# Alternating feed-forward blocks: another order within a step on TensorE, VectorE and ScalarE, squares one step later, forms at steps 9 to 20

## The chip, the cores and the metric

The kernel runs on one core of a Trainium2 chip. The metric is the device time of one execution in microseconds. A change of less than about 0.2% can't be told from none.

## What is computed

The reference is one encoder block: two gated mixing branches, an output projection and a layer norm, then a feed-forward part with a second layer norm. The change lies in the feed-forward part alone:

```python
ff = jnp.square(jax.nn.relu(h @ w_ff1[l])) @ w_ff2[l]
h = _layernorm(DEEPNORM_ALPHA * h + ff, ln2_g[l], ln2_b[l])
```
h is 256 x 2048, w_ff1 is 2048 x 8192, w_ff2 is 8192 x 2048, all float32. The kernel gets its precision by splitting each float32 operand into a high part (a cast to fp32r) and a low part (the rest), and by multiplying high x high, high x low and low x high.

## The kernel before

The hidden width of 8192 is cut into four quarters of 16 blocks of 128 channels. `ff1_first` (L1210) computes the first quarter's hidden blocks. `ff_pairs` (L1278) then runs 48 **steps** (SLOTS). Each step does two things: it computes one hidden block of the next quarter (tile f: 2048 input channels times 128 hidden channels, for 256 tokens), and it adds one pair of hidden blocks of the quarter before into the output sums (tiles w0 to w6). The last quarter's output product, and the second layer norm, follow behind the loop.

The product with w_ff2 is done in Strassen's manner: a pair of hidden blocks by 256 tokens and the matching weights form 2 x 2 blocks, and seven products replace eight. So each pair of hidden blocks needs seven sums or differences of its four parts, called **forms** (L1123; two for the weights: `plain_split` adds ring units on VectorE and by two accumulating DMAs). The seven products gather in seven PSUM tiles over eight steps, then `take_sum` (L1251) moves them out, with seven moves each 8 steps; `join_sums` (L1262) combines them at the end.

What a step holds, in the order written out by hand (`pin` keeps it on each engine; instructions that aren't pinned, DMAs and joins among them, are placed by a scheduler):

- TensorE, 53 matmuls: products 0 to 2 of the pair (`form_products(.., 0, ..)`, L1238, 9 matmuls on the weights b_h, b_l), products 3 and 4 (6 matmuls on the pair weights whi, wlo from `pair_split`), half 0 of f (8 high, 8 low), products 5 and 6 of the pair of the step before (6 matmuls on the weights in fa, from `last_split`), half 1 of f (8 low, 8 high).
- ScalarE (L1104 is the helper `cast`) makes the high parts: b_h (1024 and 512 wide), half 0 of the next block of f (whi from fraw), pair (whi from ring), last (fa from ring), then f_l (half of f's PSUM, copied out), half 1 of the next block (whi from fraw), casts for forms, and in every second step Relu and Square (`squares`, L1117) over the four parts in a tile fr.
- VectorE (L1101 is the helper `VT`) makes the low parts, called rests: b_l, b_h's end, then two sums over ring, the rest of half 0 (wlo from fraw), of pair (wlo from ring), of last (fa from ring), then the sum of f's two halves into fr (`quad_sum`, L1109), the rest of half 1, and the forms (six operations, 128 to 384 wide).

Buffers tie these together. All eight PSUM banks are in use: seven for the products and one for f, so half 0 of a step can't begin before `quad_sum` of the step before has read f. b_h and b_l have one buffer, refilled when the first nine matmuls of a step are done. The weights of half 0, pair and half 1 have one buffer each. `last_split` writes the spare end of the two fa tiles, which products 5 and 6 read; the slots of fa hold the forms of eight pairs. ring is a set of three 1 MB tiles, loaded by SyncE (`ring_load`, L1149) when `last_split` is done with the tile of three steps before; fraw is a set of two (`block_load`, L1197), reloaded behind half 1's rest. The two accumulating DMAs (L1169, ring<-wblk, and L1170, ring<-ring) are issued by GpSimd behind the two sums over ring, and `last_split` of the next step reads what they leave.

The forms of a quarter are due at steps 9 to 16 of the next (step s forms pair s - 9, at the end of the step), since a slot of fa comes free when the step before has used it a last time; in the last quarter they are plain (one cast and one rest of 512). Each tile fr is one of five.

Of the kernel before, what the change touches and what calls it, by code (L numbers as in the profile page):

```python
# [9 lines left out]
F32 = mybir.dt.float32  # L10
# [6 lines left out]
P = 128  # L17
# [26 lines left out]
def block_kernel(  # L44
# [28 lines left out]
    base = ctx.enter_context(tc.tile_pool(name="base", bufs=1))  # L73
# [20 lines left out]
    def fetch():  # L94
        n = fetched[0]
        if n >= stop_at[0]:
            return
        fetched[0] = n + 1
        raw = wp.tile([P, D], F32, tag="raw", bufs=3, name=f"raw{n}")
        nc.sync.dma_start(raw, wblk[n])  # L100
        parts = []
        for h in range(2):
            hi, lo = weight_half(n, h)
            split_hi_lo(hi, lo, raw[:, h * 1024:(h + 1) * 1024])
            parts.append((hi, lo))
        queue.append(parts)
# [31 lines left out]
    def channel_psum(name):  # L138
        return psum_main(name).rearrange("p (a b) -> p a b", a=2)

    def channel_products(ps, act, half, kts, ts=FULL, opens=True):
        hi, lo = half
        at = [(kt, slice(kt % 8 * P, (kt % 8 + 1) * P)) for kt in kts]

        def high():
            for kt, js in at:
                MM(ps[:, :, ts], hi[:, js], act[:, kt, :, ts], start=(kt == 0 and opens), stop=(kt == KT - 1))  # L147

        def low():
            for kt, js in at:  # L150
                MM(ps[:, 0, ts], lo[:, js], act[:, kt, 0, ts], start=False, stop=False)  # L151

        for part in (high, low) if kts[0] == 0 else (low, high):
            part()
# [94 lines left out]
    with tc.tile_pool(name="xp", bufs=1) as xp, tc.tile_pool(name="xq", bufs=1) as xq:  # L249
# [25 lines left out]
        for i in range(3):  # L275
            t = weight_half(-1, i)
# [198 lines left out]
    for i in range(2 * NCH):  # L475
        c, o = divmod(i, 2)
        n = 4 + (i * 21) // 15
# [23 lines left out]
    for g in range(4):  # L501
        ng = fp.tile([P, 512], F32, tag="ng", name=f"ng{g}")
        nc.scalar.dma_start(ng, norm_g[0:1, g * 512:(g + 1) * 512].broadcast_to([P, 512]))
        pss = token_group(xT, f"r{g}")
# [173 lines left out]
    for h in range(HEADS):  # L678
        v2 = yT[:, 4 * h:4 * h + 4].rearrange("p k i l -> p (k i l)").rearrange("p (i t d) -> p i t d", i=2, t=NT)
        vh, vl = v2[:, 0], v2[:, 1]  # L680
        pss = token_group(xT, f"v{h}")
# [12 lines left out]
    for g in range(4):  # L694
        pss = token_group(xT, f"g1_{g}")
# [138 lines left out]
    for s in range(NCH // 2):  # L834
        for k, n in enumerate(("v", "x1", "x2")):
            pss = token_group(xT, f"u{n}{s}")
# [27 lines left out]
    for g in range(4):  # L864
        pss = token_group(xT, f"g2_{g}")
# [20 lines left out]
    for g in range(4):  # L886
        pss = token_group(yhT, f"ho{g}")
# [93 lines left out]
    for g in range(3):  # L981
        pss = token_group(mT, f"wo{g}")
# [4 lines left out]
    pss = [[psum_main(f"wo3_{tb}{ch}") for ch in range(2)] for tb in range(NT)]  # L987
    column_products(pss, mT, [queue.popleft()], range(NT), 0)
    stop_at[0] = FF_PAIRS
    hT = act_tile(ep, "hT", "hT")  # L990
# [84 lines left out]
    def fa_slot(i):  # L1075
        if fa[1] is None:
            fa[1] = ep.tile([P, 8192], F32R, tag="f", name="fa1")
        t = fa[i // 4][:, i % 4 * 1792:(i % 4 + 1) * 1792]
        return t.rearrange("p (h k j) -> p h k j", h=2, j=P)
# [9 lines left out]
    quad_tiles = [base.tile([P, 4, P], F32, tag=t, name=f"fr{i}") for i, t in enumerate(("dfth", "dftl", "sum"))]  # L1089
    quad_tiles += [ep.tile([P, 4, P], F32, tag=f"fr{i}", name=f"fr{i}") for i in (3, 4)]  # L1090

    def quads(i):
        return quad_tiles[i % 5]

    pinned = [False]

# [12 lines left out]
    def quad_sum(i, c, ps, name):  # L1109
        low = base.tile([P, L], F32, tag="low", name=name)  # L1110
        dst = quads(i)[:, 2 * c:2 * c + 2][:, ::-1]
        halves = [a.rearrange("p (t j) -> p t j", j=P) for a in (ps[:, 0], low)]
        with tc.high_priority():
            cast(low, ps[:, 1])
            VT(dst, halves[0], halves[1], ALU.add)

    def squares(i):  # L1117
        q = quads(i)
        pin(nc.scalar.activation(q, q, AF.Relu))
        return pin(nc.scalar.activation(q, q, AF.Square))  # L1120


    def forms(i, plain=False):  # L1123
        q, slot = quads(i), fa_slot(i)
        hi, lo = slot[:, 0], slot[:, 1]
        if plain:
            cast(hi[:, 0:4], q)
            rest(lo[:, 0:4], q, hi[:, 0:4])
            return
        t = base.tile([P, 2, P], F32, tag="as", name=f"fw{i}")  # L1130
        cast(hi[:, 0:3], q[:, 1:4])
        VT(t, q[:, 0:1].broadcast_to([P, 2, P]), q[:, 1:3][:, ::-1], ALU.subtract)
        cast(hi[:, 3:5], t)
        VT(q[:, 0], q[:, 1], t[:, 0], ALU.subtract)
        rest(lo[:, 0:3], q[:, 1:4], hi[:, 0:3])
        VT(q[:, 2], q[:, 3], q[:, 0], ALU.subtract)
        cast(hi[:, 5:7], q[:, 0:3:2])
        rest(lo[:, 3:5], t, hi[:, 3:5])
        rest(lo[:, 5:7], q[:, 0:3:2], hi[:, 5:7])
# [4 lines left out]
            return fa_slot(kt // 2)[:, part, ((1, 0), (3, 2))[kt % 2][ts.start // P]]  # L1144

    SLOTS = 48

    def ring_load(p):
        nc.sync.dma_start(ring_tile(p), wblk[FF_PAIRS + 2 * p])  # L1149
# [33 lines left out]
    def pair_split(p):  # L1183
        hi, lo = weight_half(FF_PAIRS + 2 * p, 0)
        split_units(p, 1, hi, lo, raw_units(p)[:, 0:4:3])

    def last_split(p):
        fa_slot(4)
        hi, lo = (t[:, 7168:8192] for t in fa)
        split_units(p, 2, hi, lo, raw_units(p)[:, 1:3])  # L1190
# [8 lines left out]
    half_parts = {}  # L1199

    def half_split(p, h):
# [4 lines left out]
        half_parts[p, h] = (hi, lo)  # L1206
        if h and p + 2 < SLOTS:
            block_load(p + 2)
# [29 lines left out]
    def form_products(pss, p, which, ks):  # L1238
        i = p % 8
        slot = fa_slot(i)  # L1240
        for k, (wh, wl) in zip(ks, pieces_of.pop((p, which))):
            ps, f = pss[k], FORM[k]
            sh, sl = slot[:, 0, f], slot[:, 1, f]
            pin(MM(ps, sh, wh, start=(i == 0), stop=False))  # L1244
            MM(ps, sh, wl, start=False, stop=False)  # L1245
            pin(MM(ps, sl, wh, start=False, stop=(i == 7)))  # L1246
        if i == 7:
            for k in ks:
                take_sum(p // 16, p // 8 % 2, k, pss[k])

# [11 lines left out]
    def join_sums(g):  # L1262
        TT = nc.vector.tensor_tensor
        c1, c2 = slice(g * 1024, g * 1024 + 512), slice(g * 1024 + 512, g * 1024 + 1024)
        p1, p5, p6, p7 = (zacc[:, g, k] for k in range(4))
        z11, z12, z21, z22 = z1[:, 0, c1], z1[:, 0, c2], z1[:, 1, c1], z1[:, 1, c2]
        return [
            lambda: TT(z11, z11, p1, op=ALU.add),
            lambda: TT(p6, p6, p1, op=ALU.subtract),
            lambda: TT(z12, z12, p6, op=ALU.add),  # L1270
            lambda: TT(z12, z12, p5, op=ALU.add),
            lambda: TT(p6, p6, p7, op=ALU.add),
            lambda: TT(z21, z21, p6, op=ALU.subtract),
            lambda: TT(p6, p6, p5, op=ALU.add),
            lambda: nc.vector.scalar_tensor_tensor(z22, z22, ALPHA, p6, op0=ALU.mult, op1=ALU.add),
        ]

    def ff_pairs():  # L1278
        pss = [psum_side(f"w{j}") if j not in (2, 3, 4) else psum_main(f"w{j}") for j in range(7)]
        joins = []  # L1280
        for s in range(SLOTS):
            more = s + 1 < SLOTS
            pinned[0] = True
            form_products(pss, s, 0, (0, 1, 2))
            if more:
                plain_split(s + 1)
            form_products(pss, s, 1, (3, 4))
            ps = channel_psum(f"f{s // 16 + 1}_{s % 16}")
            channel_products(ps, hT, half_parts.pop((s, 0)), range(8))
            if more:  # L1290
                half_split(s + 1, 0)
                pair_split(s + 1)
            if s:
                form_products(pss, s - 1, 2, (5, 6))
                if s == SLOTS - 8:
                    joins = join_sums(0)
            last_split(s)
            if s + 2 < SLOTS:
                ring_load(s + 2)
            channel_products(ps, hT, half_parts.pop((s, 1)), range(8, 16))  # L1300
            i, c = divmod(s % 16, 2)
            quad_sum(i, c, ps, f"f{s // 16 + 1}_l{s % 16}")
            if more:
                half_split(s + 1, 1)
            if s >= 9 and (s - 9) % 16 < 8:
                forms((s - 9) % 16, s >= 2 * 16 + 9)
            if c:
                squares(i)
            if joins:
                joins.pop(0)()  # L1310
            pinned[0] = False
            if s == SLOTS - 2:
                stop_at[0] = nblk - 4
                fetched[0] = FF_PAIRS + 2 * SLOTS
            for _ in range(max(0, s - SLOTS + 3)):
                fetch()
        return pss, joins

    def ff_close(pss, joins):
        form_products(pss, SLOTS - 1, 2, (5, 6))  # L1320
        forms(7, True)
        for j in joins + join_sums(1):
            j()

# [15 lines left out]
    for g in range(3):  # L1340
        pss = [psum_main(f"w2_3{g}_{tb}") for tb in range(NT)]
# [34 lines left out]
    ps = psum_main("w2_33_0")  # L1376
    token_products([ps], f3, parts, [0], 0)
    pss = [psum_main(f"w2_33_1{ch}") for ch in range(2)]
# [16 lines left out]
    with tc.high_priority(), tc.issue_after(done.ins):  # L1395
# [3 lines left out]
        y, t, v, rs = (ep.tile([P, 1], F32, tag=f"fin{i}", name=f"fin{i}") for i in range(4))  # L1399
# [158 lines left out]
```

## Time and profile before

| | |
|---|---|
| median of 3 runs | 1818.28 us (1817.59 to 1818.85) |
| the profiled execution | 1818.21 us |
| its span, first to last instruction | 1816.4 us |
| mean granted clock of TensorE | 0.999 |
| start of step 0 of the 48, and of step 47 | 1199.34 us and 1707.06 us |
| busy: TensorE, VectorE, ScalarE | 1797.7, 1454.9, 1042.5 us |

In the profile's rows, PE is TensorE's matmuls and PEld its weight loads, DVE is VectorE, ACT is ScalarE, POOL is GpSimd and SP is SyncE; a Q behind a name is that engine's sequencer. A row of a timeline has the start and the duration in us, the engine, the line of the kernel, the operation, the tile written <- the tiles read, the shape, the count, and in brackets the idle time of the engine just before it and what ended that. A row of the waits reads: engine, tile and line that waited <- engine, tile and line that it waited for: us in total, times, longest us. A row of stretches has the stretch, its length, the busy time (and instructions) of PE, PEld, DVE, ACT and POOL, the granted clock, the busy share of the DMA engines and GB/s.

### The profile page before, as it was taken

How to read it: one execution, taken by the hardware profiler on the slowest of the kernel's cores; microseconds unless marked ns; L12 is line 12 of the kernel's file. 1: busy time of each engine (PE TensorE's matmuls, PEld its weight loads, DVE VectorE, ACT ScalarE, POOL GpSimd, SP SyncE). 2: the span in 40 equal slices, each digit the busy share in tenths (PEclk: the TensorE clock that was granted, in tenths of full speed). 3: DMA queues.
4: the chain of work that ended last, by engine and by line, in shares of the span. 5: the costliest groups of instructions: out<-in, count | busy, mean ns of one | idle time of the engine just before them, and what ended most of it. 6: DMA issues, size and time to landing. Idle time of an engine off the chain costs nothing.

```text
span 1816.4 us, 23481 instructions
## 1 busy us (share of the span) xinstructions
PE 1797.7 (99%) x8787; PEld 1505.1 (83%) x8787; DVE 1454.9 (80%) x1893; ACT 1042.5 (57%) x1423; POOL 164.8 (9%) x217
## 2 busy tenths in 40 slices
PE   9999999999999999999999999999999999999998
PEld 7888888888888888888888889888877887788887
DVE  6789887875689899988755667688889888989867
ACT  6678668865344444444544445666666566666632
POOL 1011110000111101010000000011111111111100
PEclk9999999999999999999999999999999999999999
DMA  8678876445798979797555764578777977789663
GB/s 324 227 256 292 249 230 200 149 163 204 229 297 250 308 248 283 251 278 258 197 187 186 310 235 159 187 213 248 236 227 235 275 235 221 221 255 273 214 219 127
DMA packets 79283, 424.77 MB, mean 234 GB/s; under 512 B 9817, under 2 KB 12393, under 8 KB 38465
## 3 DMA queue, kind: packets, MB, share of 16 engines
q1 hardware_dynamic: 47808, 336.61, 50.5%
q0 software_dynamic: 24304, 66.99, 18.2%
q10 hardware_dynamic: 7056, 19.67, 3.1%
q8 instruction: 69, 1.13, 0.3%
q14 instruction: 46, 0.37, 0.1%
HBM read 381.86 MB, written 16.25 MB: 219 GB/s over the span
## 4 chain that ended last, share of the span: by engine, by line
PE 87%; DVE 7%; ACT 3%; issue 3%; DMA 1%; ACTq 0%; DVEq 0%; POOL 0%
PE f L147 9%; PE f L151 5%; PE g L200 3%; PE g L199 3%; PE g L201 3%; PE ux L199 3%; PE ux L200 3%; PE ux L201 3%; PE w L1245 3%; PE w L1244 3%; PE w L1246 3%; PE k L147 2%; PE v L201 2%; PE v L200 2%; PE v L199 2%
## 5 line engine op out<-in xcount | busy, mean ns | idle before, releaser
L86 ACT CAST whi<-raw 128x1024 fp32r<-128x1024 f32 x392 | 412.7, 1055 | 408.6 <-PE ux L201 84.4
L87 DVE TENSOR_TENSOR wlo<-raw,whi 128x1024 fp32r<-128x1024 f32 x392 | 477.1, 1221 | 206.8 <-ACT whi L86 205.5
L147 PE MATMUL f<-hT,whi 128*128 128x512 f32 x984 | 246.4, 395 | 2.4 <-DVE fr L1101 1.9
L147 PEld LDWEIGHTS f<-hT,whi 128*128 128x128 f32 x984 | 180.4, 189 | 44.4 <-DVE fr L1101 10.1
L151 PEld LDWEIGHTS f<-hT,wlo 128*128 128x128 f32 x984 | 132.3, 190 | 8.7
L151 PE MATMUL f<-hT,wlo 128*128 128x256 f32 x984 | 135.0, 282 | 0.0
L1101 DVE TENSOR_TENSOR wlo<-fraw,whi 128x1024 fp32r<-128x1024 f32 x96 | 117.0, 1219 | 11.8 <-ACT whi L1104 11.8
L1169 POOL DMA_DIRECT2D ring<-wblk x48 | 41.7, 869 | 723.0 <-DVE ring L1101 723.0
L1104 ACT CAST whi<-ring 128x1024 fp32r<-128x1024 f32 x48 | 50.6, 1054 | 90.6 <-DVE ring L1101 83.8
L1104 ACT CAST whi<-fraw 128x1024 fp32r<-128x1024 f32 x96 | 100.7, 1049 | 0.2 <-PE f L147 0.2
L200 PE MATMUL g<-wlo,xT 128*128 128x512 f32 x256 | 100.1, 391 | 0.0
L201 PE MATMUL ux<-whi,xT 128*128 128x512 f32 x256 | 99.9, 390 | 0.0
L201 PE MATMUL g<-whi,xT 128*128 128x512 f32 x256 | 99.8, 390 | 0.0
L200 PE MATMUL ux<-wlo,xT 128*128 128x512 f32 x256 | 99.6, 389 | 0.0
L199 PE MATMUL g<-whi,xT 128*128 128x512 f32 x256 | 93.8, 392 | 0.0
L199 PE MATMUL ux<-whi,xT 128*128 128x512 f32 x256 | 89.7, 389 | 0.0
L1101 DVE TENSOR_TENSOR b_l<-ring,b_h 128x1024 fp32r<-128x1024 f32 x48 | 58.7, 1224 | 33.1 <-ACT b_h L1104 33.0
L1104 ACT CAST b_h<-ring 128x1024 fp32r<-128x1024 f32 x96 | 74.9, 829 | 8.8 <-ACT whi L1104 8.2
L1101 DVE TENSOR_TENSOR ring<-ring 128x512 f32<-128x512 f32 x96 | 66.0, 688 | 1.6
L1101 DVE TENSOR_TENSOR wlo<-ring,whi 128x1024 fp32r<-128x1024 f32 x48 | 58.8, 1225 | 2.7 <-ACT whi L1104 1.2
L1101 DVE TENSOR_TENSOR fa<-ring,fa 128x1024 fp32r<-128x1024 f32 x48 | 58.5, 1219 | 0.8 <-ACT fa L1104 0.8
L1104 ACT COPY f_l<-f 128x256 f32<-128x256 f32 x64 | 23.7, 370 | 61.1 <-PE f L147 58.2
(538 smaller groups left out, 4345.4 us busy)
## 6 DMA issues: line engine op xcount, KB each, us to landing
raw<-wblk SPq DMA_DIRECT2D x204, 1024.0 KB, 5.1
fraw<-wblk SPq DMA_DIRECT2D x48, 1024.0 KB, 7.1
ring<-wblk SPq DMA_DIRECT2D x48, 1024.0 KB, 6.2
Td<-T POOLq DMA_DIRECT2D x32, 384.0 KB, 5.4
conv_sb<-conv_rows SPq DMA_DIRECT2D x12, 1024.0 KB, 11.5
Tl<-Td POOLq DMA_DIRECT2D x16, 768.0 KB, 9.4
ring<-wblk POOLq DMA_DIRECT2D x48, 256.0 KB, 4.3
ring<-ring POOLq DMA_DIRECT2D x48, 256.0 KB, 5.0
```

Source lines behind the costliest of these rows:

```text
L86: return (nc.scalar.copy(hi, src), nc.vector.tensor_tensor(lo, src, hi.bitcast(F32), op=ALU.subtract))
L87: nc.vector.tensor_tensor(lo, src, hi.bitcast(F32), op=ALU.subtract))
L147: MM(ps[:, :, ts], hi[:, js], act[:, kt, :, ts], start=(kt == 0 and opens), stop=(kt == KT - 1))
L151: MM(ps[:, 0, ts], lo[:, js], act[:, kt, 0, ts], start=False, stop=False)
L199: MM(pss[tb], sh, wh, start=(kt == 0), stop=False)
L200: MM(pss[tb], sh, wl, start=False, stop=False)
L201: MM(pss[tb], sl, wh, start=False, stop=(kt == KT - 1))
L1101: return pin(nc.vector.tensor_tensor(dst, a, b, op=op))
L1104: return pin(nc.scalar.copy(hi, src))
L1244: pin(MM(ps, sh, wh, start=(i == 0), stop=False))
L1245: MM(ps, sh, wl, start=False, stop=False)
L1246: pin(MM(ps, sl, wh, start=False, stop=(i == 7)))
```

## The change

Within a step, TensorE does products 0 to 2, 3 and 4, 5 and 6 (of the step before), then both halves of f. VectorE and ScalarE do plain, last, pair, half 0, forms, the sum of f, half 1, in this order; before it was plain, half 0, pair, last, the sum of f, half 1, forms. Relu and Square of a pair go from the end of its step to the next step, behind half 0's cast. The forms of a quarter go from steps 9 to 16 (one each) to steps 9, 10, 12, 14, 15, 17, 18 and 20; those of the last quarter that fall behind the loop are made in `ff_close`. `take_sum` is called behind plain, behind pair and behind the forms, instead of right after the products. The joins of the first half begin a step later in the text; they aren't pinned, and in the built program they begin in step 39 in both kernels. The number of instructions of each kind is the same.

```diff
-    def forms(i, plain=False):
-        q, slot = quads(i), fa_slot(i)
+    def forms(n):
+        q, slot, plain = quads(n), fa_slot(n % 8), n >= 24
...
+    FORMED = {16 * (q - 1) + s: 8 * q + i for q in range(1, 4) for i, s in enumerate((9, 10, 12, 14, 15, 17, 18, 20))}
...
-        if i == 7:
+
+    def take_sums(pss, p, ks):
+        if 0 <= p < SLOTS and p % 8 == 7:
             for k in ks:
                 take_sum(p // 16, p // 8 % 2, k, pss[k])
...
         for s in range(SLOTS):
             more = s + 1 < SLOTS
+            n, c = divmod(s + 16, 2)
             pinned[0] = True
             form_products(pss, s, 0, (0, 1, 2))
+            form_products(pss, s, 1, (3, 4))
+            if s:
+                form_products(pss, s - 1, 2, (5, 6))
+            ps = channel_psum(f"f{s // 16 + 1}_{s % 16}")
+            for h in range(2):
+                channel_products(ps, hT, half_parts.pop((s, h)), range(8 * h, 8 * h + 8))
+            if s + 2 < SLOTS:
+                ring_load(s + 2)
             if more:
                 plain_split(s + 1)
-            form_products(pss, s, 1, (3, 4))
-            ps = channel_psum(f"f{s // 16 + 1}_{s % 16}")
-            channel_products(ps, hT, half_parts.pop((s, 0)), range(8))
+            take_sums(pss, s, (0, 1, 2))
+            last_split(s)
+            if more:
+                pair_split(s + 1)
+            take_sums(pss, s, (3, 4))
             if more:
                 half_split(s + 1, 0)
-                pair_split(s + 1)
-            if s:
-                form_products(pss, s - 1, 2, (5, 6))
-                if s == SLOTS - 8:
-                    joins = join_sums(0)
-            last_split(s)
-            if s + 2 < SLOTS:
-                ring_load(s + 2)
-            channel_products(ps, hT, half_parts.pop((s, 1)), range(8, 16))
-            i, c = divmod(s % 16, 2)
-            quad_sum(i, c, ps, f"f{s // 16 + 1}_l{s % 16}")
+            if c == 0 and s:
+                squares(n - 1)
+            if FORMED.get(s, 0) >= 8:
+                forms(FORMED[s])
+            take_sums(pss, s - 1, (5, 6))
+            quad_sum(n, c, ps, f"f{s // 16 + 1}_l{s % 16}")
             if more:
                 half_split(s + 1, 1)
-            if s >= 9 and (s - 9) % 16 < 8:
-                forms((s - 9) % 16, s >= 2 * 16 + 9)
-            if c:
-                squares(i)
+            if s == SLOTS - 7:
+                joins = join_sums(0)
             if joins:
                 joins.pop(0)()
             pinned[0] = False
...
+        squares(31)
         return pss, joins
 
     def ff_close(pss, joins):
         form_products(pss, SLOTS - 1, 2, (5, 6))
-        forms(7, True)
+        take_sums(pss, SLOTS - 1, (5, 6))
+        for s in range(SLOTS, SLOTS + 8):
+            if s in FORMED:
+                forms(FORMED[s])
```

More of the change, by code (lines that the diff above doesn't have):

```diff
@@ L1090, in block_kernel, with quads @@
     quad_tiles += [ep.tile([P, 4, P], F32, tag=f"fr{i}", name=f"fr{i}") for i in (3, 4)]
-    def quads(i):
-        return quad_tiles[i % 5]
+    def quads(n):
+        return quad_tiles[n % 5]
     pinned = [False]
@@ L1115, in quad_sum, with squares @@
             VT(dst, halves[0], halves[1], ALU.add)
-    def squares(i):
-        q = quads(i)
+    def squares(n):
+        q = quads(n)
         pin(nc.scalar.activation(q, q, AF.Relu))
         return pin(nc.scalar.activation(q, q, AF.Square))
-    def forms(i, plain=False):
-        q, slot = quads(i), fa_slot(i)
+    def forms(n):
+        q, slot, plain = quads(n), fa_slot(n % 8), n >= 24
         hi, lo = slot[:, 0], slot[:, 1]
@@ L1129, in forms @@
             return
-        t = base.tile([P, 2, P], F32, tag="as", name=f"fw{i}")
+        t = base.tile([P, 2, P], F32, tag="as", name=f"fw{n}")
         cast(hi[:, 0:3], q[:, 1:4])
```

## The prediction

> **What bounds the kernel now.** I read the page's first block, then the stretches of the 48-step loop, the waits from 1120 us on, and the timelines of TensorE (PE), VectorE (DVE) and ScalarE (ACT) in one step without forms and in steps with them.
>
> ```profile
> span 1816.4 us, 23481 instructions
> PE 1797.7 (99%) x8787; PEld 1505.1 (83%) x8787; DVE 1454.9 (80%) x1893; ACT 1042.5 (57%) x1423; POOL 164.8 (9%) x217
> ```
> ```profile
> 1208.30:1301.42 93.12, 93.12 (x478) 79.71 (x477) 78.40 (x87) 59.79 (x76) 17.12 (x20) 1.00 0.87 256
> 1311.77:1404.46 92.69, 88.02 (x426) 69.59 (x424) 82.74 (x119) 61.73 (x91) 15.23 (x18) 1.00 0.76 226
> 1487.23:1582.44 95.21, 89.36 (x425) 70.64 (x424) 85.03 (x123) 59.76 (x87) 15.21 (x18) 0.98 0.74 221
> 1634.18:1655.33 21.15, 21.15 (x107) 17.56 (x106) 21.04 (x28) 11.91 (x16) 2.50 (x5) 1.00 0.85 248
> ```
> ```profile
> PEld w L1245 <- DVE wlo L1101: 12.2, 15, 2.1
> PEld f L147 <- DVE fr L1101: 10.1, 18, 1.7
> ```
> The kernel is TensorE's: 99%. The columns of the second fence are the stretch, its length, busy time (instructions) of PE, PEld, DVE, ACT and POOL, the clock, the DMA share and GB/s. The first stretch is steps 1 to 9, without forms; a step has 53 matmuls (478 / 9), and lasts 93.12 / 9 = 10.347 us. The next two are steps 11 to 18 and 27 to 34 (424 weight loads = 8 x 53), the last is steps 40 and 41. At 10.347 they would last 82.77, 82.77 and 20.69. So 9.92 + 12.44 + 0.46 = **22.8 us** is waiting, and it lies around the forms. The waits name two things: the low part of the two pair weights (wlo, 12.2 us), and the sum of the two halves of f (fr, 10.1 us), which frees the only PSUM buffer that the next block of f can have.
>
> One step without forms, first PE (starts of its groups), then DVE and ACT:
>
> ```profile
> 1253.09 1.98 PE L147 MATMUL f<-hT,whi 128*128 128x512 f32 x8
> 1254.90 1.11 PE L151 MATMUL f<-hT,wlo 128*128 128x256 f32 x8
> 1255.86 0.40 PE L1244 MATMUL w<-fa,fa 128*128 128x512 f32 x1
> ...
> 1257.24 1.11 PE L151 MATMUL f<-hT,wlo 128*128 128x256 f32 x8
> 1258.20 2.00 PE L147 MATMUL f<-hT,whi 128*128 128x512 f32 x8
> 1260.04 0.39 PE L1244 MATMUL w<-b_h,fa 128*128 128x512 f32 x1
> ```
> ```profile
> 1250.30 0.42 DVE L1101 TENSOR_TENSOR fr<-f,f_l 128x256 f32<-128x256 f32 x1 [0.52 <-ACT f_l L1104]
> 1251.24 1.23 DVE L1101 TENSOR_TENSOR wlo<-fraw,whi 128x1024 fp32r<-128x1024 f32 x1 [0.52 <-ACT whi L1104]
> 1253.06 1.23 DVE L1101 TENSOR_TENSOR b_l<-ring,b_h 128x1024 fp32r<-128x1024 f32 x1 [0.59 <-ACT b_h L1104]
> 1254.20 0.69 DVE L1101 TENSOR_TENSOR b_h<-ring,b_h 128x512 fp32r<-128x512 f32 x1
> 1254.80 1.42 DVE L1101 TENSOR_TENSOR ring<-ring 128x512 f32<-128x512 f32 x2
> 1256.13 1.22 DVE L1101 TENSOR_TENSOR wlo<-fraw,whi 128x1024 fp32r<-128x1024 f32 x1
> 1257.40 1.23 DVE L1101 TENSOR_TENSOR wlo<-ring,whi 128x1024 fp32r<-128x1024 f32 x1
> 1258.57 1.23 DVE L1101 TENSOR_TENSOR fa<-ring,fa 128x1024 fp32r<-128x1024 f32 x1
> 1260.70 0.42 DVE L1101 TENSOR_TENSOR fr<-f,f_l 128x256 f32<-128x256 f32 x1 [0.90 <-ACT f_l L1104]
> ```
> ```profile
> 1256.31 1.06 ACT L1104 CAST whi<-ring 128x1024 fp32r<-128x1024 f32 x1 [1.81 <-DVE ring L1101]
> ```
> The step began at 1260.04 - 10.35 = 1249.69. From there: 15 products to 3.40 (0.227 each), half 0 of f to 6.17, six products of the step before to 7.55, half 1 to 10.35. On DVE the pitch from start to start is 1.14 for a 1024-wide rest, 0.60 for 512, 1.33 for both ring sums. DVE is idle only in gaps: here 2.0 us.
>
> With forms, DVE in three steps running:
>
> ```profile
> 1331.58 1.23 DVE L1101 TENSOR_TENSOR b_l<-ring,b_h 128x1024 fp32r<-128x1024 f32 x1 [1.71 <-ACT b_h L1104]
> ...
> 1338.19 0.42 DVE L1101 TENSOR_TENSOR fr<-f,f_l 128x256 f32<-128x256 f32 x1
> 1338.52 1.21 DVE L1101 TENSOR_TENSOR wlo<-fraw,whi 128x1024 fp32r<-128x1024 f32 x1
> 1339.66 0.42 DVE L1101 TENSOR_TENSOR fw<-fr 128x256 f32<-128x256 f32 x1
> ...
> 1341.66 0.42 DVE L1101 TENSOR_TENSOR fa<-fr,fa 128x256 fp32r<-128x256 f32 x1
> 1342.62 1.23 DVE L1101 TENSOR_TENSOR b_l<-ring,b_h 128x1024 fp32r<-128x1024 f32 x1 [0.53 <-ACT b_h L1104]
> ...
> 1354.82 1.22 DVE L1101 TENSOR_TENSOR b_l<-ring,b_h 128x1024 fp32r<-128x1024 f32 x1 [1.71 <-ACT b_h L1104]
> ```
> Forms take 2.35 us of DVE (1339.66 to 1341.66, plus 0.35 until the next could start). They stand behind half 1's rest, and ACT, which casts for them, reaches b_h late: the step lasts 11.04 (1331.58 to 1342.62), and 12.20 (to 1354.82) where Relu and Square stand ahead of b_h too. DVE and ACT in lockstep set the pace there, and PE waits.
>
> **The change, part by part.** Work is the same; every removed instruction comes back elsewhere. The three PE groups of products now stand together, so f starts at 21 x 0.227 = 4.77 of a step instead of 3.40. That moves the deadline of the f sum from 13.75 to 15.1 (offsets from the start of its own step). The pair weights' low part is still needed behind ten products of the next step, at 10.35 + 2.27 = 12.6. Relu and Square go behind half 0's cast, where ACT is idle. Forms go ahead of the f sum, into the gap where DVE waits for PE's last matmul.
>
> I place the new DVE order by the same pitches, in a step without forms: b_l 3.37 (1253.06 - 1249.69), ring sums to 6.44, last rest 6.44, pair rest 7.70 (its cast starts at 6.62 and takes 1.06), half 0 rest 8.85, free at 9.99; f sum at 11.01, half 1 rest 11.95 (0.94 behind, as at 1250.30 and 1251.24), free 13.09, next b_l 13.72. The gaps are 1.02 + 0.61 + 0.63 = 2.26. With forms: 9.99 to 12.34, f sum, then 0.56 of waiting for half 1's cast (ACT casts forms, f_l, then half 1), half 1 rest at 13.24, next b_l at 14.38. So a step with forms makes DVE later by 0.66, and one without makes good up to 2.26. The f sum ends at 12.76 + lag, the pair rest at 8.93 + lag: the step bears a lag of **2.3 us** ahead of the forms before PE waits for the sum, and 3.7 for the pair.
>
> - Steps 9 to 20: the lag is 0.66 and 1.32 after 9 and 10, 0 after 11, 0.66 after 12, 0 after 13, 0.66 after 14. In 15 two sums leave PSUM on DVE (1.2), lag 1.86 at the forms; after 16 0.9, after 17 and 18 2.2, after 19 0. Never over 2.3: **0 left of 9.92**.
> - Steps 25 to 36: as before to step 31, where five sums leave PSUM on DVE, at 0.60 each:
>
> ```profile
> 1645.44 1.28 DVE L1101 TENSOR_TENSOR zr<-zr,w 128x512 f32<-128x512 f32 x2
> ```
>   That is 3.0 us in one step with forms: lag 3.66, PE waits 1.4. Two more in 32; 33 and 34 with forms leave 0.3. **1.7 left of 12.44.**
> - Steps 39 to 42: seven sums and eight joins again (15 x 0.6 = 9 us), now with pair behind last: pair 0.8 late in 41. **0.8 left**, where 0.46 was.
> - Close: the three forms behind the loop are plain (0.6 each), and one of five sums is behind the next weights: **0.2**.
> - Steps without forms keep 10.35: squares, casts and loads lie beside PE. PE's own work is unchanged; uncovered, the squares would cost 1.2 (12.20 - 11.04) in every second step.
>
> One cost the trace does not show directly. Last rest stood at 8.88 (1258.57); now it comes first, at 6.44, so its cast, 1.12 ahead, needs the two accumulating DMAs at 5.3 of the step behind their issue instead of 7.8. If they are late, ACT stands at that cast, with the casts of pair and half 0 queued behind it, and DVE stands at last rest. And ring's load, which SP issues when last rest ends, now goes out 1.2 us behind the ring sums and not 3.7 (1259.80 against 1256.13), upon those DMAs. The load behind half 1's rest stays where it was.
>
> ```profile
> 1256.92 0.87 POOL L1169 DMA_DIRECT2D ring<-wblk  x1 [8.37 <-DVE ring L1101]
> 1257.46 1.22 POOL L1170 DMA_DIRECT2D ring<-ring  x1
> ```
> ```profile
> DMA to landing us min/median/max: 4.7/5.0/10.6
> ```
> ```profile
> DMA to landing us min/median/max: 9.2/9.2/9.2
> ```
> The second fence is all 48 of ring<-ring, the third the one issued at 1412.32. It is issued 1.33 behind the ring sums (1256.13, 1257.46), now at 7.8, and has 10.35 + 5.3 - 7.8 = 7.9 us with the lag unchanged (8.5 as it grows, 5.6 to 7.2 where it just fell). At 5.0 nothing is late, and nothing earlier can help; at 9.2 it is late behind every recovery and the windows are lost again. So the cost lies between 0 and 20. I take a flight of about 7 us and **1.0 us**, nearer the median, since most of this data moves ahead of ring's.
>
> By the Trainium skill (DMA: Bandwidth & Descriptors, Queues, rings and completion order) each DMA engine takes turns between its queues packet by packet, so the two would share rather than queue; that rule speaks against this order, and the rival below is its mechanism. The trace agrees only so far that the landings spread from 4.7 to 10.6.
>
> Sum: -22.8 + 1.7 + 0.8 + 0.2 + 1.0 = -19.1. The profiled execution took 1818.2 (span 1816.4 and 1.8 around it; the median of the three runs is 1818.28), so **1799.1 us**.
>
> **Rivals.**
> - *Accumulates late by sharing.* At 8.3 to 9.2 us every recovery step is followed by a late last rest, each step with forms behind one waits 1.3 to 1.8, and 6 to 16 us stay: 1804 to 1814. For it: the DMA share is already 0.87. Against: the median of 5.0.
> - *No gain:* DVE has 12 x 8.09 + 8 x 2.92 + 4.2 = 124.7 us of work in 12 steps of 124.2. If a form costs 0.5 more in lockstep than I read, nothing is made good and the stalls only move: 1815 to 1822.
> - *Slower:* from one accumulate's landing to the issue of the second next, DVE and ACT need last cast 1.12, then last 1.26, pair 1.15, half 0 1.14, f sum 0.33, half 1 1.14, b_l 1.14, b_h 0.60, ring 1.33, issue 1.33 = 10.5 (8.1 before, when pair and half 0 came ahead of last). With the flight that must fit into two steps, 20.7: from **10.2 us** of flight on every step is longer. At the 10.6 of the largest row it is 0.4 for each of 23 pairs of steps, 9 us, with the 22.8 back: about 1827. Against: one of 48 took that long.
> - *The change doesn't do what it says:* only the joins and the last three forms are free for the scheduler; the order of the built program holds the rest as written. No chance of its own.
>
> **How the numbers follow.** Forecast 1796 to 1804: 0.63. Late accumulates, 1804 to 1814: 0.19. Better than 1796 (about all 22.8 gone): 0.04. No gain: 0.08. Slower: 0.06. Within 0.2% is 3.6 us, about what a measurement can tell from no change. Faster 0.86, same 0.08, slower 0.06. The range 1795 to 1811 leaves out no gain (0.08), slower (0.06), the end of the late accumulates (0.04) and what lies below 1795 (0.02).
>
> **What would show it.** Steps 9 to 20 at 10.35 each; the wait of PEld for wlo gone and that for fr under 3 us, at steps 32 and 34; ring<-ring landing at a median of 6 to 7.5; ACT's fa cast seldom waiting for it. Wrong would be: fa waiting for ring<-ring by many us in total, or b_l more than 0.7 later in each step with forms.

## The result, and the profile after

The changed kernel takes **1836.0 us** (median of 4 runs, 1835.47 to 1837.52) against 1817.99 (4 runs, 1817.59 to 1818.85): a ratio of 1.0100, 95% interval 1.0082 to 1.0117. It is 1% slower, where 1799.1 was forecast and a range up to 1811. The profiled execution took 1836.46 us.

The page's first block, then the stretches, with the columns of the stretches of before. The first is steps 1 to 9, then come steps 11 to 18, 27 to 34, 40 and 41, and one more, steps 37 to 46:

```profile
span 1834.0 us, 23436 instructions
PE 1798.0 (98%) x8787; PEld 1506.7 (82%) x8787; DVE 1451.3 (79%) x1893; ACT 1041.3 (57%) x1423; POOL 164.9 (9%) x217
```
```profile
1211.68:1305.81 94.13, 93.24 (x478) 79.68 (x477) 77.60 (x87) 60.40 (x78) 16.92 (x20) 1.00 0.88 253
1316.14:1406.42 90.28, 84.97 (x425) 70.33 (x424) 75.49 (x104) 56.55 (x81) 12.79 (x15) 1.00 0.80 233
1492.37:1585.01 92.64, 85.11 (x425) 70.24 (x424) 79.00 (x109) 55.62 (x79) 13.84 (x17) 1.00 0.80 227
1642.96:1665.38 22.42, 21.50 (x107) 17.49 (x106) 22.38 (x30) 11.10 (x16) 2.02 (x3) 1.00 0.83 233
1606.57:1724.40 117.83, 108.89 (x531) 89.69 (x530) 97.28 (x118) 70.85 (x93) 17.60 (x20) 0.97 0.78 225
```
A step in which nothing is late now lasts 10.33 us. Above that, steps 11 to 18 hold 90.28 - 82.64 = 7.6 us of waiting (9.9 before) and steps 27 to 34 hold 10.0 (12.4 before). So some of the forecast gain is there. But steps 37 to 46, which have four plain forms, now hold 117.83 - 103.3 = 14.5 us (0.5 before); one of them, step 43, lasts 17.22. From the start of step 0 to that of step 47 the loop takes 521.68 us, against 507.72. Most of the rest of the longer span, 3.4 us, lies in the opening loads, ahead of everything that was changed: the loop begins at 1202.72 instead of 1199.34. In the trace of a near repeat of the kernel (below) it begins at 1198.98, so the 3.4 us don't come from the change.

The waits from 1120 us on (total us, times, longest), and the landings of all 48 ring<-ring, the second accumulating DMAs (the time from issue to landing is called the flight below):

```profile
ACT fa L1105 <- DMA ring<-ring: 107.0, 27, 9.3
DVE fa L1102 <- ACT fa L1105: 55.8, 21, 6.5
PEld f L147 <- DVE fr L1102: 15.5, 13, 1.8
PEld w L1247 <- DVE wlo L1102: 12.2, 13, 1.3
```
```profile
DMA to landing us min/median/max: 4.9/8.4/13.2
```
This is the picture that the prediction named as "wrong": last's cast waits for the second accumulating DMA 27 times, 107 us in all (once, 1.0 us, before), and VectorE stands behind the cast for 56. The landing went from a median of 5.0 us to 8.4. One late landing, first ACT, then DVE, then the queue of POOL and that of SP:

```profile
1351.02 1.58 ACT L1105 CAST b_h<-ring 128x1024 fp32r<-128x1024 f32 x2
1359.70 1.05 ACT L1105 CAST fa<-ring 128x1024 fp32r<-128x1024 f32 x1 [7.10 <-DMA ring<-ring]
1360.65 1.04 ACT L1105 CAST whi<-ring 128x1024 fp32r<-128x1024 f32 x1
```
```profile
1354.33 1.41 DVE L1102 TENSOR_TENSOR ring<-ring 128x512 f32<-128x512 f32 x2
1360.78 1.22 DVE L1102 TENSOR_TENSOR fa<-ring,fa 128x1024 fp32r<-128x1024 f32 x1 [5.05 <-ACT fa L1105]
...
1370.30 1.41 DVE L1102 TENSOR_TENSOR ring<-ring 128x512 f32<-128x512 f32 x2
```
```profile
1348.94 1.22 POOL L1172 DMA_DIRECT2D ring<-ring  x1
...
1372.78 1.22 POOL L1172 DMA_DIRECT2D ring<-ring  x1
```
```profile
1348.88 0.33 SPq L1151 DMA_DIRECT2D ring<-wblk  x1
```
```profile
DMA to landing us min/median/max: 10.7/10.7/10.7
```
The last fence is the accumulate issued at 1348.94. It lands at about 1359.6, 0.1 us before the cast that has waited 7.10 us for it. SP issued ring's 1 MB load in the same instant, 0.06 us ahead. From the landing to the issue at 1372.78, the second next, there are 13.2 us of ACT and DVE work. With the flight that makes 23.8 us for two steps, which should last 20.7.

### The profile page after: what moved, and what is told of

Its sections match the earlier page's. It is cut to its first block, busy times and chain, and to the rows that moved or that the text cites. A ratio compares the mean times of both kernels' runs of the same rounds, so it can differ in the third digit from the quotient of the medians.

```text
span 1834.0 us, 23436 instructions
## 1 busy us (share of the span) xinstructions
PE 1798.0 (98%) x8787; PEld 1506.7 (82%) x8787; DVE 1451.3 (79%) x1893; ACT 1041.3 (57%) x1423; POOL 164.9 (9%) x217
## 4 chain that ended last, share of the span: by engine, by line
PE 80%; DVE 8%; DMA 7%; issue 2%; ACT 2%; POOL 0%; ACTq 0%; SPq 0%; DVEq 0%; POOLq 0%
PE f L147 6%; DMA ring<-ring 6%; PE f L151 3%; PE g L200 3%; PE g L199 3%; PE g L201 3%; PE ux L201 3%; PE ux L199 3%; PE ux L200 3%; DVE wlo L1102 2%; PE w L1247 2%; PE w L1248 2%; PE w L1246 2%; PE r L199 2%; PE r L201 2%
## 5 line engine op out<-in xcount | busy, mean ns | idle before, releaser
L151 PEld LDWEIGHTS f<-hT,wlo 128*128 128x128 f32 x984 | 126.1, 191 | 4.8
L1102 DVE TENSOR_TENSOR wlo<-fraw,whi 128x1024 fp32r<-128x1024 f32 x96 | 117.0, 1219 | 13.6 <-ACT whi L1105 13.5
L151 PE MATMUL f<-hT,wlo 128*128 128x256 f32 x984 | 127.7, 283 | 0.0
L1105 ACT CAST fa<-ring 128x1024 fp32r<-128x1024 f32 x48 | 50.5, 1052 | 113.8 <-DMA ring<-ring 107.0
```

The lines of the kernel that those rows point to most:

```text
L1102: return pin(nc.vector.tensor_tensor(dst, a, b, op=op))
L1105: return pin(nc.scalar.copy(hi, src))
```

## Experiments

Theory A: ring's load, released by last rest right behind the ring sums, shares the DMA engines with the accumulates; they land late, and last's cast now comes first. Theory B: the early deadline is enough, whatever the flight. Theory C: forms and squares in their new place make ACT and DVE slower in lockstep. The kernels were made from the changed one, and the last four from the one with half 0 first. The edits are shown shortened, without the lines between that stay and without the conditions at the end of the loop.

### 1. Last behind, and pair ahead of last

```
 plain_split(s + 1)
-last_split(s); pair_split(s + 1); half_split(s + 1, 0)
+pair_split(s + 1); half_split(s + 1, 0); last_split(s)     # first kernel
+pair_split(s + 1); last_split(s); half_split(s + 1, 0)     # second kernel
```


> The changed kernel, with only the rest of the last pair of blocks put back behind the pair and half 0 (order on VectorE and ScalarE: plain, pair, half 0, last; the order on TensorE, the squares and the forms as in the changed kernel). Theory A (the load of ring, released by last rest right behind the ring sums, shares the DMA engines with the two accumulates, which then land too late for the cast that now comes first): ring's load goes out 3.5 us behind the ring sums again, ring<-ring lands at a median of 5.0 to 5.5 us, the waits of ACT for ring<-ring fall from 107 us to under 3, and the time is 1797 to 1801 us, or up to 1804 if the 3.4 us lost ahead of the loop belong to the kernel. Theory B (only the early deadline matters, not the sharing): the same time, 1797 to 1804, as the deadline is late here too. Theory C (the new place of the forms and squares makes ACT and DVE slower in lockstep): 1815 to 1836, with the waits turned into waits between DVE and ACT.

> The changed kernel with the pair's rest ahead of last's (plain, pair, last, half 0): last's deadline and the release of ring's load both come 1.15 us later than in the changed kernel. Theory A: ring's load goes out about 2.4 us behind the ring sums (1.2 in the changed kernel, 3.7 in the kernel before), ring<-ring lands at a median of 5.2 to 7, with 9 us to land in, and few casts are late: 1797 to 1808 us. Theory B: the deadline is later by 1.15 us of the 2.5 that were lost, so about half of the loss stays: 1812 to 1822. Theory C: 1815 to 1836.

Measured: 1818.69 (ratio to the kernel before 1.0006, interval 0.9997 to 1.0014) and 1818.32 (1.0001, 0.9992 to 1.0010). The landings and the waits for them went about as theory A said (medians 4.8 and 5.3; no wait in the first kernel, 0.7 us in the second), but the time did not. The second lies in the ranges of theories B and C, yet hardly a cast waits for a DMA in it, which B needs. In the first kernel, the landings of ring<-ring, two waits, and one step without forms on DVE and ACT:

```profile
DMA to landing us min/median/max: 4.4/4.8/9.9
```
```profile
ACT whi L1105 <- DVE ring L1102: 146.1, 46, 6.6
DVE wlo L1102 <- ACT whi L1105: 63.3, 74, 1.5
```
```profile
1264.85 1.42 DVE L1102 TENSOR_TENSOR ring<-ring 128x512 f32<-128x512 f32 x2
1267.45 1.23 DVE L1102 TENSOR_TENSOR wlo<-ring,whi 128x1024 fp32r<-128x1024 f32 x1 [1.19 <-ACT whi L1105]
```
```profile
1266.37 1.05 ACT L1105 CAST whi<-ring 128x1024 fp32r<-128x1024 f32 x1 [2.78 <-DVE ring L1102]
```
No cast waits for a DMA. But the pair's cast needs the ring sums, so DVE stands 1.2 us behind them, in 40 of 48 steps, until that cast is done. A step had 2.26 us of gaps by the prediction's count; over half is gone, and the lag of the forms isn't made good. So theory A was not the whole story. I added **theory D**: whatever stands first behind the ring sums must have its cast done by then. Half 0 can (it needs only fraw), last can if its accumulates have landed, the pair can't.

### 2. The load of ring held back

```
 if s + 2 < SLOTS:
-    ring_load(s + 2)
+    with tc.issue_after(held[0].ins):      # half 0's rest, one step before
+        ring_load(s + 2)
```


> The changed kernel with every instruction in its order; the load of ring alone is held back until half 0's rest is done, 2.4 us later than last rest releases it. Theory A: ring<-ring lands at a median of 5.0 to 6.0 us, ACT's waits for it fall from 107 us to under 10, and the time is 1797 to 1803 us. Theory B (the early deadline of last's cast, whatever the flight): the waits for ring<-ring stay at 60 us or more and the time is within 0.3% of the changed kernel, 1830 to 1840. Theory C: 1815 to 1836 with short landings.

Measured: 1835.75 us, ratio 1.0100 (1.0086 to 1.0113), landings 4.9/8.5/13.5. The trace shows why: in 22 steps of the loop the load goes out less than 0.6 us behind the accumulate, or ahead of it, and so it does in 22 steps of the changed kernel. The edit set no wait here. It tells nothing of theory A, but it nearly repeats the changed kernel; its loop begins at 1198.98 us, not 1202.72, and takes 523.6 us. The next two kernels make the load really wait, by a read of one column of its buffer:

```
     half_split(s + 1, 0)                   # or behind pair_split
+    t = ring_tile(s)[:, 1023:1024]
+    VT(touched, t, t, ALU.add)
```


> The changed kernel, with one addition of one column of the ring buffer on VectorE behind half 0's rest, into a tile that nothing reads: ring's load has to wait for that read, so it really goes out 2.4 us later than last rest releases it (in the kernel with the load held, the trace shows it going out 0.1 to 0.5 us behind the second accumulate as before: that edit set no wait, and it counts as a repeat of the changed kernel). Order and deadlines are the changed kernel's. Theory A (sharing with ring's load makes the accumulates late): ring<-ring lands at a median of 5 to 6 us, ACT's waits for it fall from 107 us to under 10, and the time is 1796 to 1802 us. Theory B (the early deadline of last's cast is enough): the waits stay at 50 us or more and the time at 1820 to 1840.

> The same read, put behind the pair's rest: ring's load goes out 1.2 us later than in the changed kernel. Theory A: between the changed kernel and the one held until half 0; ring<-ring lands at a median of 5.5 to 7.5 us, some casts wait, 1797 to 1815 us. Theory B: 1820 to 1840.

Measured: **1799.09** with the read behind half 0 (ratio 0.9897, 0.9880 to 0.9913), 1816.06 with it behind the pair (0.9983, 0.9974 to 0.9993). The same step in the changed kernel and in the first of these, the issues of the second accumulate and of ring's load, and the landing of that accumulate:

```profile
1251.45 1.25 POOL L1172 DMA_DIRECT2D ring<-ring  x1
```
```profile
1251.54 0.33 SPq L1151 DMA_DIRECT2D ring<-wblk  x1
```
```profile
DMA to landing us min/median/max: 8.8/8.8/8.8
```
```profile
1246.02 1.25 POOL L1172 DMA_DIRECT2D ring<-ring  x1
```
```profile
1248.63 0.33 SPq L1151 DMA_DIRECT2D ring<-wblk  x1
```
```profile
DMA to landing us min/median/max: 5.1/5.1/5.1
```
The accumulate is issued 7.60 us into its step in both. The load is 0.09 us behind it in the changed kernel and 2.61 in the other, and the flight falls from 8.8 to 5.1. Over the loop, with the read behind half 0:

```profile
DMA to landing us min/median/max: 4.4/5.1/10.6
```
```profile
ACT fa L1105 <- DMA ring<-ring: 12.1, 5, 6.7
```
One read of 0.15 us per step, which is work added, brings back 37 us: theory A holds, theory B falls, since the order and the deadline are the changed kernel's. The waits are a little over the 10 us expected; more than half of them, 6.7, is one cast, in step 43, which the last paragraph on the prediction takes up. Behind the pair the load of this step comes 1.4 us later instead of 2.5, and the landings stay at a median of 7.7 with 80 us of waits: a little outside what I expected. I sorted the second accumulates of eight kernels' loops (before, changed, last behind, pair first, the two with half 0 first of the fourth section, the two with a read; 360 rows) by how long after them ring's load was issued. Up to 1.6 us: 84 rows, none under 7.5. From 1.6 to 2.2: 16 rows, median 5.5. Beyond 2.2: 260 rows, medians 5.2 (up to 3.0) and 5.3 (beyond). It is not a slope but nearly a step.

By the Trainium skill (DMA: Bandwidth & Descriptors, Queues, rings and completion order), each DMA engine serves the queues in turn, packet by packet. The pair of rows above agrees so far: a load issued behind an accumulate delays it by 3.7 us, which it could not if they went one after the other.

### 3. No accumulates

```
-nc.gpsimd.dma_start(u[1], wblk[n, :, 1536:2048], accum_op=ALU.add)
-nc.gpsimd.dma_start(u[2], u[3], accum_op=ALU.add)
```


> The changed kernel without the two accumulating DMAs of each step, so that the sums of the last pair of blocks lack two of their terms; everything else is as in the changed kernel. It bounds what the accumulates cost in all. Theories A and B: no wait for them, steps 9 to 20 at 10.33 us, and what is left is what the prediction left for the other parts (2.7 us): 1796 to 1801 us, or up to 1804 with the 3.4 us ahead of the loop. Theory C: 1815 to 1836.

Without them the sums of the last pair lack two terms, so this kernel only bounds what the accumulates cost. Measured: 1796.68 us, ratio 0.9886 (0.9871 to 0.9901). Its stretches 9 to 20, 25 to 36 and 37 to 46:

```profile
1290.12:1414.04 123.92, 123.92 (x638) 106.33 (x636) 114.44 (x155) 86.92 (x122) 0.00 (x0) 1.00 0.58 203
1455.34:1580.81 125.47, 124.40 (x637) 106.18 (x636) 117.48 (x160) 84.89 (x119) 0.00 (x0) 1.00 0.57 201
1580.81:1684.58 103.77, 103.63 (x532) 88.53 (x530) 94.59 (x116) 67.74 (x88) 0.00 (x0) 1.00 0.56 203
```
At 10.33 a step they would last 123.96, 123.96 and 103.3. Nothing is lost in the first, 1.5 in the second, 0.5 in the third. So theory C falls, and everything else in the change is worth what was forecast. What the changed kernel loses hangs on the accumulates: 1836.0 - 1796.7 = 39.3 us by the medians. In the traces the loop shows 521.7 - 486.0 = 35.7 us of it (37.6 in the near repeat).

### 4. Half 0 first

```
 plain_split(s + 1)
-last_split(s); pair_split(s + 1); half_split(s + 1, 0)
+half_split(s + 1, 0); pair_split(s + 1); last_split(s)     # first kernel
+half_split(s + 1, 0); last_split(s); pair_split(s + 1)     # second kernel
```


> The changed kernel with the order of the splits as it was before the change (plain, half 0, pair, last); the order on TensorE, the squares and the forms stay as in the changed kernel. In the kernel with pair first the profile showed VectorE idle 1.19 us behind the ring sums in every step, since the pair's cast can only start when they are done. Theory A with that (theory D: what stands first behind the ring sums must have its cast done by then, and the accumulates must have room): half 0's cast is done early, VectorE runs on, ring<-ring lands at a median of 5 us, and the time is 1796 to 1801 us. Rival (half 0's two weight buffers are still read by TensorE, which now comes to half 0 1.4 us later in the step, so its cast waits): VectorE is idle about 1 us behind the ring sums again, 1815 to 1820.

> The changed kernel with the order plain, half 0, last, pair: last's cast is due 1.15 us later than in the changed kernel, and ring's load goes out 2.4 us behind the ring sums. Theory A with D: ring<-ring lands at a median of 5 to 6 us, no cast waits for it, and the time is 1796 to 1801 us. Rival (half 0's buffers come free late): 1815 to 1820, with ACT's cast of half 0 waiting for TensorE.

Measured: **1797.36** (ratio 0.9884, 0.9869 to 0.9899) and 1800.74 (0.9903, 0.9888 to 0.9917). The first is the changed kernel with only the splits put back in the order of before. Its stretches 9 to 20 and 25 to 36 lose nothing and 1.7 us:

```profile
1291.91:1415.86 123.95, 123.95 (x637) 106.28 (x636) 114.39 (x154) 85.98 (x123) 21.10 (x24) 1.00 0.85 252
1457.17:1582.84 125.67, 124.49 (x638) 106.16 (x637) 117.47 (x160) 83.95 (x119) 21.11 (x24) 1.00 0.85 250
```
Theory D holds, and the rival (half 0's buffers) doesn't bear. The second kernel came out in time as expected, but not for the reason given: its landings are as long as the changed kernel's.

```profile
DMA to landing us min/median/max: 5.1/8.2/9.9
```
```profile
ACT fa L1105 <- DMA ring<-ring: 54.0, 27, 5.0
DVE fa L1102 <- ACT fa L1105: 13.4, 12, 3.1
```
ACT waits 54 us for the accumulates, yet DVE stands for only 13.4, since it has half 0's rest to do meanwhile and last is due 1.15 us later. So the long flight alone costs some 3 us. It takes both: the load right behind the accumulate **and** last's cast at the head of the queues.

### 5. What each other part is worth

Each of these undoes one part in the kernel with half 0 first (1797.36 us).

```
-if FORMED.get(s, 0) >= 8: forms(FORMED[s])       # ahead of the f sum
 half_split(s + 1, 1)
+if FORMED.get(s, 0) >= 8: forms(FORMED[s])
```


> The kernel with half 0 first (the changed kernel with the splits in the order plain, half 0, pair, last: 1797.4 us), with the forms put back behind half 1's rest, in the same steps. It asks what the place of the forms ahead of the f sum is worth. The prediction's reading: behind half 1 the gap of 1.02 us in which VectorE waits for the f sum is not used, so each step with forms makes VectorE later by about 1.7 us instead of 0.66; then steps 9, 10, 14, 15, 17 and 18 run over the 2.3 us that the f sum bears, and 5 to 12 us of waiting of TensorE come back: 1802 to 1810 us. Rival (the later place of the f sum on TensorE is enough by itself): 1796 to 1800 us.

```
-form_products(pss, s - 1, 2, (5, 6))
 channel_products(ps, hT, half_parts.pop((s, 0)), range(8))
+form_products(pss, s - 1, 2, (5, 6))
 channel_products(ps, hT, half_parts.pop((s, 1)), range(8, 16))
```


> The kernel with half 0 first, with the order on TensorE as before the change (half 0 of f ahead of the six products of the last pair). f's first matmul comes 1.37 us earlier in a step, so the f sum bears a lag of 0.9 us instead of 2.3. By the lags worked out in the prediction (1.32 after step 10, 1.9 in step 15, 2.2 after steps 17 and 18) TensorE waits 2 to 3.5 us in each of the two windows with forms: 1800 to 1806 us. Rival (the order on TensorE is worth nothing, the order on VectorE did it all): 1796 to 1799 us.

```
-if c == 0 and s: squares(n - 1)                  # behind the last of the splits above
 half_split(s + 1, 1)
+if c: squares(n)
```


> The kernel with half 0 first, with Relu and Square put back to the end of the step that ends their quad, behind half 1's rest. By the prediction they cost 1.2 us where they are not covered, in the steps with forms (9, 15, 17 of each window), since ScalarE then reaches b_h's cast late; steps without forms have the slack. 3 to 8 us come back: 1800 to 1806 us. Rival (ScalarE has slack there now, as the forms' casts are ahead): 1796 to 1799 us.

Measured: 1800.90 (forms, +3.5), 1801.88 (TensorE, +4.5) and 1802.43 (squares, +5.1); ratios to the kernel before 0.9905 (0.9889 to 0.9922), 0.9909 (0.9895 to 0.9924) and 0.9915 (0.9900 to 0.9930). The largest wait of TensorE for VectorE in each (a line of the waits from 1120 us on), in this order:

```profile
PEld w L1247 <- DVE wlo L1102: 4.8, 7, 1.1
```
```profile
PEld f L147 <- DVE fr L1102: 6.4, 7, 2.8
```
```profile
PEld f L147 <- DVE fr L1102: 5.6, 5, 1.7
```
The intervals of these ratios overlap with that of the kernel with half 0 first (0.9869 to 0.9899), but the loops in the traces say the same: 490.35, 491.98 and 492.36 us against 486.26. All three rivals fall: each part is worth 3 to 6 of the 20.6 us between this kernel and the one before. The forms gave less than the 5 to 12 us that I had worked out. The three add up to 13.1 (15.9 of 21.5 by the loops); the other 7.5 must come when more than one of them is undone, or with the moved sums and joins, which wasn't tried.

```
-(9, 10, 12, 14, 15, 17, 18, 20)
+(9, 10, 11, 13, 14, 17, 18, 20)
```


> The kernel with half 0 first, with the forms at steps 9, 10, 11, 13, 14, 17, 18, 20 instead of 9, 10, 12, 14, 15, 17, 18, 20, so that none is in the step in which five sums leave PSUM (15 and 31). The prediction left 1.4 us of waiting at step 32 for it, and the trace of the kernel with half 0 first shows 1.5. By the lags it should go (lag 1.32 + 3.0 - 2.26 = 2.1, under 2.3): step 32 at 10.3 to 10.5 us in the trace instead of 11.84, 1795 to 1798 us, a difference in the time that a measurement can hardly tell. Rival: three steps with forms running (9, 10, 11) go over the 2.3 us, and 0.5 us or more comes back at step 12 and 28.

Measured: 1796.47 us, ratio 0.9881 (0.9866 to 0.9896). Its stretch of steps 25 to 36:

```profile
1456.70:1581.65 124.95, 124.27 (x637) 106.18 (x636) 117.67 (x161) 84.49 (x119) 21.10 (x24) 1.00 0.85 254
```
1.0 us is lost there instead of 1.7, all of it in step 32 (11.36 instead of 11.84, not the 10.3 to 10.5 expected); nothing is late at 12 and 28. In time it can't be told from the kernel with half 0 first. These two are the fastest kernels here that compute the whole result.

## Why the prediction was wrong, step by step

- **What bounds the kernel: right.** 22.8 us of waiting around the forms was to be had. Without accumulates the loop takes 486.04 us instead of 507.72, with them and half 0 first 486.26.
- **The new order on VectorE: right.** In the kernel without accumulates, which has the changed kernel's order, steps 9 to 12 begin at 1290.12, 1300.44, 1310.77 and 1321.10, and b_l starts at

```profile
1293.44 1.23 DVE L1102 TENSOR_TENSOR b_l<-ring,b_h 128x1024 fp32r<-128x1024 f32 x1 [0.55 <-ACT b_h L1105]
...
1304.37 1.22 DVE L1102 TENSOR_TENSOR b_l<-ring,b_h 128x1024 fp32r<-128x1024 f32 x1
...
1315.34 1.22 DVE L1102 TENSOR_TENSOR b_l<-ring,b_h 128x1024 fp32r<-128x1024 f32 x1
...
1324.46 1.23 DVE L1102 TENSOR_TENSOR b_l<-ring,b_h 128x1024 fp32r<-128x1024 f32 x1 [0.53 <-ACT b_h L1105]
```
  that is 3.32, 3.93, 4.57 and 3.36 into them: 0.61 and 0.64 of lag per step with forms (0.66 forecast), made good by one step without. What is left, 1.5 in steps 25 to 36 and 0.5 in 37 to 46, was forecast as 1.7 and 0.8.
- **The flight of the accumulates: the step that failed.** "I take a flight of about 7 us and 1.0 us ... since most of this data moves ahead of ring's." It doesn't: with the load up to 1.6 us behind, no second accumulate landed in under 7.5, and the median of the changed kernel is 8.4. The text had the order and the 1.2 us behind the ring sums right, but took 7, between the median of before (5.0) and its row of 9.2. In before the load was 2.5 us behind the accumulate (median), and in no row of its loop less than 2.0, so that median said nothing of the new place. One row of before did, with another load: the longest, 10.6, which the text set aside as one of 48. There ACT issues a load of 1 MB from ln_rows 0.55 us behind the accumulate, and ring's load follows only at 2.81 (the three issues, then the accumulate's landing):

```profile
1655.29 1.24 POOL L1170 DMA_DIRECT2D ring<-ring  x1
```
```profile
1655.84 0.34 ACTq L907 DMA_DIRECT2D zr<-ln_rows  x1
```
```profile
1658.10 0.33 SPq L1149 DMA_DIRECT2D ring<-wblk  x1
```
```profile
DMA to landing us min/median/max: 10.6/10.6/10.6
```
- **The bound of 20 us: also wrong.** The term measured 39.3 by the medians, 36 to 38 in the loops of two traces. I let the cost end where the windows with forms were lost again. But a late landing also makes later steps late that had nothing to recover: 14.5 us in steps 37 to 46 alone.
- **The rivals.** "Late by sharing" had the flight (8.3 to 9.2) and the mechanism, and priced it by that same bound, 6 to 16 us. "Slower" had the chain that decides, landing to second next issue, with 10.5 us of work. Where last's cast was waiting, the trace of the changed kernel gives 10.3 to 10.8 from step 10 on if the step between has no forms, and 13.2 to 13.3 if it has the six operations: the 2.35 us of forms were left out. (For accumulates of steps 2 to 7, where DVE stood for other things too, it is 11.1 to 13.0; among the plain forms 11.4 to 12.0.) So the flight from which a chain with forms makes steps longer is 20.7 - 13.2 = 7.5 us, not 10.2, and the median of 8.4 lies beyond it. (VectorE's work in "no gain" adds up to 124.6 us, not 124.7; nothing hangs on it.) The accumulates issued in steps 3 to 9 fly for up to 9.0 us, and with no forms in most of their chain steps 3 to 12 keep their 10.33.
- **A cost not seen:** that the pair can't stand first behind the ring sums. It played no part in the changed kernel, where last stands there, but it decided the first two experiments.
- **"What would show it"**: steps 9 to 12 ran at 10.33 as forecast; the wait for fr rose instead of falling under 3 us, the one for wlo stayed at 12.2, and fa waited for ring<-ring for 107 us.

The longest step, 43, follows the longest flight (13.2), with ring's load issued 0.06 us ahead of the accumulate and that of ln_rows 0.6 behind. With ring's load 2.8 to 2.9 us behind and ln_rows' 0.54, the same accumulate flies 10.5 us with half 0 first and 10.6 with the read behind half 0; in the latter it is the 6.7 us of waiting, and step 43 lasts 12.48. So the load of ln_rows seems to do to an accumulate what ring's does, and neither half 0 first nor the held load shortens that flight. This is argued from the issue times, since no run moved that load alone. Nor was it tried what in the DMA engines or memories makes the flight jump at 1.6 us.

## What to carry to other kernels

When a reordering releases a transfer earlier, look at what is in flight at that moment: a large load issued right behind a small DMA that somebody waits for can make the small one much longer (here 8.5 us instead of 5.3, with the load up to 1.6 us behind), and the median of a trace in which the two never met says nothing about it. Put what waits for a DMA, or for the instruction just before it, not first in an in-order queue, but behind work whose input is long there. Where a lateness is handed from one iteration to the next, price it over the whole loop, with the heaviest iteration's work in the chain.

## What the runs showed of the hardware

- An accumulating DMA of 256 KB from SBUF to SBUF takes a median of 5.2 to 5.3 us where the next 1 MB load of ring, on another queue, is issued over 2.2 us behind it (260 rows), and 7.5 to 13.2 where it is issued up to 1.6 us behind (84 rows). Since it reads nothing from HBM, it isn't only HBM that they share. Nor is it late only because it stands behind the first accumulate, which does read HBM and is issued 0.5 us ahead of it: with the load 0.5 to 1.6 us behind the second, the first takes a median of 4.3 us, as it does with the load beyond 2.2, and the second 8.3 (62 rows).
- The load is slowed too: in the changed kernel it lands in 7.25 us (median of 32) when issued up to 1.6 us behind the accumulate, and in 4.8 (median of 13) when later. Without any accumulates its median is 4.8. In the kernel before, some 2.5 us behind, it takes 6.2 (median of 45), though the accumulates there take 5.0; what holds it up there wasn't tried.
